# Neighbourhood attention in an order written by hand, with the DeltaNet's branch product as filler work

## The chip, the cores and the metric

One core of one Trainium2 chip. The metric is the device time of one execution in microseconds (us), the median of several runs. The core has five engines that run their own instruction queues in order: TensorE (PE, matrix products, with its weight loads listed apart as PEld), VectorE (DVE), ScalarE (ACT), GpSimd (POOL) and SyncE (SP, which only issues transfers here). ACT and POOL issue transfers too.

## The reference

One layer of a flow-matching model, D_MODEL = 1024, for T = 640 tokens: 128 context tokens and 512 latent tokens on a grid of 8 rows by 64 columns. In every layer a DeltaNet branch and an attention branch read the same normalised input, and their outputs are merged:

```python
def _merge(o_na, o_dn, z, gate_na, gate_dn, dn_norm, w_ao, w_do, w_out):
    o_dn = _rms(o_dn, dn_norm) * jax.nn.silu(z).reshape(B, T, DN_HEADS, DN_DV)
    br_na = o_na.reshape(B, T, NA_WIDTH) @ w_ao
    br_dn = o_dn.reshape(B, T, DN_V_WIDTH) @ w_do
    m = jax.nn.sigmoid(gate_na) * br_na + jax.nn.sigmoid(gate_dn) * br_dn
    return m @ w_out
```

The attention has 8 heads of 64. A context token attends to the 128 context tokens. A latent token attends to a window of 8 rows by 16 columns of the grid, with a relative bias, and to 128 cached context keys, under one softmax. Queries and keys of the latent tokens are rotated by their grid position first. A feed-forward part (squared ReLU, hidden width 4096) follows. All is float32.

## The kernel before

Every dense product is done as three products of float32r parts: `hi*hi + hi*lo + lo*hi`, so a weight is loaded (`load_raw`, SP), copied to `whi` (`S.copy`, ACT) and subtracted to `wlo` (DVE). What the text calls a step is three matmuls with one weight tile.

The order of instructions comes in two ways. Inside `tc.manual_schedule(engines={...})` the named engines keep the order of the program text. Elsewhere a planner orders each engine's instructions from its own model of their durations.

The DeltaNet's recurrence is in the first kind. It goes in slots: `slot(...)` runs a part of the recurrence and then takes steps from a generator `dense()` until 2.4 nominal us are reached (a step is counted as its columns at full clock). `dense()` goes through units of projection weights listed in `FILL`: `v` (values), `q` (queries and keys), `g` (gates, 16 units of 16 steps of 320 columns), with `m` and `a` small extras. A function can be put off by some slots with `later(slots, phase, f)`, run by `do(phase)`; the phases of a slot are "mid", "end", "post". After the last recurrence step the slots go on until all units are done (L1123). Each of the last two steps has a normalisation of the DeltaNet's output (`finish_o`: squares, norms, product, transposes `turned`, store to `od_d` in DRAM).

Then comes the attention, ordered by the planner. Its loops go over four pairs of heads `hp` and five blocks `b`: four latent blocks of 128 queries, which are 16 columns by 8 rows, with 256 window keys and 128 cached ones, and one context block. A pair's two heads lie in the partitions 0 to 63 and 64 to 127. Per head and block: scores into PSUM (L1207 and L1209; L1212 for the context block), the bias added and the minimum found in one DVE instruction (L1227; the scores are negated, so this is the softmax's maximum), the exponential with its sum (ACT, L1231), the reciprocal (L1232) and the normalisation (DVE, L1233), three transposes by PE (L1236) and their copy to `pT` (ACT, L1238). Then the values of both heads (L1250) and the split of the output into `aoh` and `aol`. The rotations of queries and keys are DVE instructions (L1181 to L1192), with the products with the tables on POOL for all pairs but the first. POOL also negates the bias. Values `vw` are loaded by SP, queries, keys and bias by ACT.

The branch products are two passes over `w_br`: i = 1 is the DeltaNet's (reads `doh`, `dol`; L1309 writes `dop`), i = 0 the attention's (reads `aoh`, `aol`), which also adds the two and splits the sum for the next product. Each pass has four weight tiles of two halves, and for each half 384 and 256 columns. All three lines L202, L203, L204 are the helper `mm3`. The planner puts the first pass among the attention; the second pass follows the attention, and the product with `w_out` follows that.

Of the kernel before, what the change touches and what calls it, by code (L numbers as in the profile page):

```python
# [18 lines left out]
P = 128  # L19
D = 1024  # L20
KT = 8
# [7 lines left out]
FILL = ("qv", "vqmqmqmqmqmqmqmgmgagagagagagagaggagggggg")  # L29
# [68 lines left out]
def body(ctx: ExitStack, tc: tile.TileContext, I, O, dbg=None):  # L98
# [47 lines left out]
    def newton_rsqrt(pool, x, n, tag, post=1.0):  # L146

        y = pool.tile([P, n], F32, tag=tag + "y", name=tag + "y")
        t = pool.tile([P, n], F32, tag=tag + "t", name=tag + "t")
        i = pool.tile([P, n], I32, tag=tag + "i", name=tag + "i")  # L150
# [730 lines left out]
    def finish_o(ot, hv, rq, rq2, home):  # L881

        def squares():
# [5 lines left out]
            later(len(home) > 2, "end", lambda: norms(fz, zt))  # L889

        def norms(fz, zt):
            s8 = tk.tile([P, 8], F32, tag="fs8", name="fs8", bufs=2)
            V.tensor_reduce(s8, h8(fz), axis=AX.X, op=ALU.add)
            V.tensor_tensor(s8, s8, rq2, op=ALU.mult)
            V.tensor_scalar(s8, s8, EPS, None, op0=ALU.add)
            rs = newton_rsqrt(tk, s8, 8, "fo")
            V.tensor_tensor(rs, rs, rq, op=ALU.mult)
            later(1, "end", lambda: product(rs, zt))

        def product(rs, zt):  # L900
            V.tensor_tensor(h8(zt), h8(zt), bch(rs), op=ALU.mult)
            hold[2] = V.tensor_tensor(ot, ot, zt, op=ALU.mult).ins
            later(4 if len(home) == 2 else 3 if home else 1, "mid", lambda: turned(zt))
# [15 lines left out]
    class Unit:  # L919
        def __init__(self, ch, i):  # L920
            self.ch, self.i, self.extra = ch, i, []
            self.src = I[dict(v="w_v", q="w_qk", g="w_gate")[ch]][i]
# [9 lines left out]
        def sub(self):  # L932
            for raw, (hi, lo) in zip(self.raw, self.w):
                V.tensor_tensor(lo, raw, hi.bitcast(F32), op=ALU.subtract)  # L934
            kt = 4 if self.ch == "v" else 8
# [7 lines left out]
        def out(self, g, ps, n):  # L943
# [10 lines left out]
            else:  # L954
                hp, mi = i // 2, i % 2
                S.activation(y, ps, AF.Copy, scale=(-0.125 if mi == 0 else 1.0))
# [5 lines left out]

        def run(self):
            for g in range(5 if self.ch == "v" else 2):
# [38 lines left out]
    cnts = dict.fromkeys("vqgma", 0)  # L1003
    prs, elims, plan = [], [], {}
    hold = [None] * 4
    now = [0]
# [4 lines left out]
    def do(phase):  # L1011
        for f in plan.pop((now[0], phase), ()):
            f()
# [16 lines left out]
    def dense():  # L1030
        for j, u in enumerate(us):
            if j + 1 < len(us):
                us[j + 1].load_extra()
            if j + 3 < len(us):
                us[j + 3].load()
            if j + 1 < len(us):
                us[j + 1].cast()
                later(0, "post", us[j + 1].sub)
# [7 lines left out]
    with tc.manual_schedule(engines={E_.PE, E_.DVE, E_.Activation, E_.SP}):  # L1046
# [36 lines left out]
        for n in range(5):  # L1083
            P0, P1, P2 = [preps[i] if i < 5 else none for i in (n, n + 1, n + 2)]
# [37 lines left out]
        raw3[0] = None  # L1122
        while slot() or plan:  # L1123
            pass
# [16 lines left out]

    with (
        tc.tile_pool(name="at0", bufs=2, side="right", reuse_waits="tile") as at0,
        tc.tile_pool(name="at", bufs=2, side="right", reuse_waits="tile") as at,
    ):
        def load_vw(hp):
            vw = at0.tile([P, 4, 2, 256], F32, tag="vw", name="vw", bufs=1)
            for b in range(4):
                for kt in range(2):
                    nc.sync.dma_start(vw[:, b, kt], v_rc[4 * kt : 4 * kt + 4, W0[b] : W0[b] + 32, hp * 128 : hp * 128 + 256])  # L1150
            return vw

        W0 = (0, 8, 24, 32)
        v_rc = v_d.rearrange("t p e -> (t p) e")[128:640].rearrange("(r c) e -> r c e", c=64)
        vw = load_vw(0)
        rope = at0.tile([P, 1024], F32, tag="rope", name="rope", bufs=1)
        nc.scalar.dma_start(rope, I["rope"])
        ckT = at0.tile([P, HP, 128], F32, tag="ckT", name="ckT", bufs=1)
        nc.scalar.dma_start(ckT, I["ckT"])
        cvt = at.tile([P, 512], F32, tag="cvt", name="cvt", bufs=1)  # L1160
        nc.scalar.dma_start(cvt, I["cv"])
        vctx = at.tile([P, 512], F32, tag="vctx", name="vctx", bufs=1)
        nc.scalar.dma_start(vctx, v_d[0])
        bias = [(at0, at)[i // 2].tile([P, 384], F32, tag=f"bias{i}", name=f"bias{i}", bufs=1) for i in range(4)]
        for b in bias:
            V.memset(b[:, 256:384], 0.0)
        swap = [16 + i for i in range(16)] + list(range(16))
        bi, bth = [0, 1], [None, None]
        for hp in range(HP):
            if hp == 2:  # L1170
                vw = load_vw(2)
            RE = V if hp == 0 else G

            rx = ExitStack()
            for ins in hold[2 * hp : 2 * hp + 2]:
                rx.enter_context(tc.issue_after(ins))
            for mi in range(2):
                x = at0.tile([P, T], F32, tag=f"qk{mi}", name=f"qk{mi}", bufs=(1, 2)[mi])
                nc.scalar.dma_start(x, qk_d[hp, mi])
                xs = at0.tile([P, 512], F32, tag="xs", name="xs", bufs=1)  # L1180
                V.stream_shuffle(xs, x[:, 128:640], swap)  # L1181
                V.tensor_tensor(xs, xs, rope[:, 512:1024], op=ALU.mult)
                if mi == 0:
                    qb = at0.tile([P, T], F32, tag="qb", name="qb")
                    S.copy(qb[:, 0:128], x[:, 0:128])
                    RE.tensor_tensor(x[:, 128:640], x[:, 128:640], rope[:, 0:512], op=ALU.mult)
                    V.tensor_tensor(qb[:, 128:640].rearrange("p (b r c) -> p r b c", r=8, b=4),
                                    x[:, 128:640].rearrange("p (r b c) -> p r b c", r=8, b=4),
                                    xs.rearrange("p (r b c) -> p r b c", r=8, b=4), op=ALU.add)
                else:  # L1190
                    RE.tensor_tensor(x[:, 128:640], x[:, 128:640], rope[:, 0:512], op=ALU.mult)
                    V.tensor_tensor(x[:, 128:640], x[:, 128:640], xs, op=ALU.add)  # L1192
                    kT = x
            rx.close()
            oh_g, ol_g = [x[:, hp, 128:640].rearrange("p (r b c) -> p b r c", r=8, b=4) for x in (brh[0], brl[0])]


            for b in range(5):
                nk = 384 if b < 4 else 128
                nj = nk // 128  # L1200
                hh = [slice(0, 64), slice(64, 128)]
                sps = [ps_tp() for _ in range(2)]
                if b < 4:
                    for hs, ps in zip(hh, sps):
                        kg = kT[hs, 128:640].rearrange("p (r c) -> p r c", r=8)
                        lq = qb[hs, 128 + 128 * b : 256 + 128 * b]
                        PE.matmul(ps[:, 0:256].rearrange("p (r c) -> p r c", r=8), lq, kg[:, :, W0[b] : W0[b] + 32], start=True, stop=True)  # L1207
                    for hs, ps in zip(hh, sps):
                        PE.matmul(ps[:, 256:384], qb[hs, 128 + 128 * b : 256 + 128 * b], ckT[hs, hp, :], start=True, stop=True)  # L1209
                else:  # L1210
                    for hs, ps in zip(hh, sps):
                        PE.matmul(ps[:, :128], qb[hs, 0:128], kT[hs, 0:128], start=True, stop=True)  # L1212
                pTs = []
# [646 lines left out]
```

## Time and profile before

| what | us |
|---|---|
| median of 3 runs (1145.94 to 1147.84) | 1147.3 |
| the profiled execution | 1145.61 |
| its span, first to last instruction | 1143.7 |
| PE busy | 1076.5 (94%) |
| PE weight loads busy | 947.5 (83%) |
| DVE busy | 862.4 (75%) |
| ACT busy | 525.7 (46%) |
| POOL busy | 306.6 (27%) |

The mean granted clock of PE was 0.986 of full speed. The last recurrence step of the DeltaNet ends on PE at about 489 us from the span's start, the last attention matmul is at 623.4, and the attention's branch product runs from 625.6 to 660.5. Busy shares of PE are to be read with care: matmuls are pipelined, a listed duration is a matmul's latency, and the distance of two starts is what it costs.

### The profile page before, as it was taken

To read this page: it belongs to the slowest core of one execution; us is meant where nothing else is said; L and a number is where in the kernel's file an instruction comes from. 1 tells how busy PE (TensorE), PEld (TensorE's weight loads), DVE (VectorE), ACT (ScalarE), POOL (GpSimd) and SP (SyncE) were. 2 spreads that over 40 slices of the span, in tenths; PEclk is the share of its full clock that TensorE was granted. 3 is DMA by queue.
4 is the path that set the end of the run, shared out by engine and by line. 5 is a ranking of instruction groups with operands and counts; after the bars stand their busy time and mean duration, and the time that the engine had idled before them with its cause. 6 is when DMAs were issued, how large, how long until landed. Compare 5 with 4: busy or idle time off the path is not lost.

```text
span 1143.7 us, 25017 instructions
## 1 busy us (share of the span) xinstructions
PE 1076.5 (94%) x10016; PEld 947.5 (83%) x10016; DVE 862.4 (75%) x1687; ACT 525.7 (46%) x1154; POOL 306.6 (27%) x238
## 2 busy tenths in 40 slices
PE   4999999989989899989999999999999999999996
PEld 2779999878867788877877999998989888897975
DVE  6567897596777777577655667699798989879785
ACT  5435443426353553434446353476444454444532
POOL 1352312000000000003220405435353534535213
PEclk9998999999989999998999999999999999999999
DMA  8831114555654544566333562446555565665605
GB/s 306 307 125 56 26 37 141 191 179 196 192 194 155 190 129 156 153 192 195 93 104 131 193 258 93 129 117 179 147 148 166 148 163 154 164 165 146 177 28 148
DMA packets 75061, 176.39 MB, mean 154 GB/s; under 512 B 16952, under 2 KB 31048, under 8 KB 74944
## 3 DMA queue, kind: packets, MB, share of 16 engines
q1 hardware_dynamic: 57136, 134.60, 35.2%
q0 software_dynamic: 4928, 15.08, 7.8%
q10 hardware_dynamic: 12880, 25.10, 6.9%
q8 instruction: 79, 1.29, 0.5%
q14 instruction: 38, 0.31, 0.1%
HBM read 150.63 MB, written 24.12 MB: 153 GB/s over the span
## 4 chain that ended last, share of the span: by engine, by line
PE 68%; DVE 17%; DMA 6%; ACT 4%; issue 3%; SPq 0%; POOL 0%; DVEq 0%; ACTq 0%; POOLq 0%
PE ps_mm L968 5%; PE ps_mm L970 4%; PE ps_mm L969 4%; DVE wlo L183 4%; PE ps_mm L203 3%; PE ps_mm L202 3%; PE ps_mm L204 3%; PE ps_mm L1460 3%; PE ps_mm L1458 2%; PE ps_mm L1459 2%; DVE y L523 2%; DVE R L1571 2%; PE ps_st L1460 2%; PE ps_st L1458 2%; PE ps_st L1459 2%
## 5 line engine op out<-in xcount | busy, mean ns | idle before, releaser
L968 PE MATMUL ps_mm<-hhi,whi 128*128 128x320 f32 x384 | 128.7, 335 | 7.7 <-ACT gth L947 4.0
L970 PE MATMUL ps_mm<-hhi,wlo 128*128 128x320 f32 x384 | 119.9, 312 | 2.0 <-DVE wlo L934 2.0
L969 PE MATMUL ps_mm<-hlo,whi 128*128 128x320 f32 x384 | 119.8, 312 | 0.0
L182 ACT CAST whi<-raw 128x1024 fp32r<-128x1024 f32 x89 | 92.3, 1046 | 39.3 <-PE ps_mm L1459 7.3
L183 DVE TENSOR_TENSOR wlo<-raw,whi 128x1024 fp32r<-128x1024 f32 x66 | 86.6, 1322 | 25.5 <-ACT whi L182 25.1
L968 PEld LDWEIGHTS ps_mm<-hhi,whi 128*128 128x128 f32 x384 | 73.5, 191 | 21.6 <-ACT gth L947 8.7
L1223 POOL TENSOR_SCALAR bias<-bias 128x256 f32<-128x256 f32 x24 | 22.1, 927 | 226.6 <-DMA bias<-in_bias_dram 210.0
L183 POOL TENSOR_TENSOR wlo<-raw,whi 128x1024 fp32r<-128x1024 f32 x23 | 56.1, 2442 | 84.6 <-ACT whi L182 84.6
L970 PEld LDWEIGHTS ps_mm<-hhi,wlo 128*128 128x128 f32 x384 | 73.3, 191 | 2.3 <-DVE wlo L934 2.3
L969 PEld LDWEIGHTS ps_mm<-hlo,whi 128*128 128x128 f32 x384 | 73.5, 191 | 0.1
L202 PE MATMUL ps_mm<-hhi,whi 128*128 128x320 f32 x192 | 60.9, 317 | 0.0
L203 PE MATMUL ps_mm<-hlo,whi 128*128 128x320 f32 x192 | 60.6, 316 | 0.0
L204 PE MATMUL ps_mm<-hhi,wlo 128*128 128x320 f32 x192 | 60.1, 313 | 0.0
L183 DVE TENSOR_TENSOR wlo<-S,whi 128x1024 fp32r<-128x1024 f32 x28 | 54.8, 1973 | 3.9 <-ACT whi L182 3.9
L183 DVE TENSOR_TENSOR wlo<-T,whi 128x1024 fp32r<-128x1024 f32 x28 | 44.0, 1570 | 15.3 <-ACT whi L182 15.3
L659 POOL DMA_DIRECT2D rls<-ai_d x10 | 5.1, 510 | 181.5 <-PE ps_tb L622 167.9
L934 DVE TENSOR_TENSOR wlo<-raw,whi 128x1024 fp32r<-128x1024 f32 x28 | 34.2, 1226 | 23.1 <-ACT whi L930 22.7
L182 ACT CAST whi<-T 128x1024 fp32r<-128x1024 f32 x28 | 29.4, 1049 | 33.4 <-PE ps_mm L1459 15.8
L523 DVE SCALAR_TENSOR_TENSOR y<-cvb,cw,y 128x644 f32<-128x644 f32 x48 | 42.6, 887 | 0.9
L182 ACT CAST whi<-S 128x1024 fp32r<-128x1024 f32 x28 | 28.9, 1051 | 22.3 <-PE ps_tb L204 10.7
L947 ACT ACTIVATE gth<-ps_mm 128x320 f32<-128x320 f32 x32 | 13.8, 435 | 51.5 <-PE ps_mm L970 42.3
L202 PEld LDWEIGHTS ps_mm<-hhi,whi 128*128 128x128 f32 x192 | 36.7, 191 | 0.8 <-ACT cvb L519 0.3
(576 smaller groups left out, 3580.7 us busy)
## 6 DMA issues: line engine op xcount, KB each, us to landing
raw<-in_w_ff_dram SPq DMA_DIRECT2D x57, 512.0 KB
raw<-in_w_ada_dram SPq DMA_DIRECT2D x48, 512.0 KB
raw<-in_w_gate_dram SPq DMA_DIRECT2D x16, 512.0 KB
S<-in_w_ff_dram SPq DMA_DIRECT2D x14, 512.0 KB
T<-in_w_ff_dram SPq DMA_DIRECT2D x14, 512.0 KB
S<-in_w_ff_dram POOLq DMA_DIRECT2D x14, 512.0 KB, 5.5
T<-in_w_ff_dram POOLq DMA_DIRECT2D x14, 512.0 KB, 7.3
raw<-in_w_dn_dram SPq DMA_DIRECT2D x12, 512.0 KB
```

Source lines behind the costliest of these rows:

```text
L182: S.copy(hi, raw)
L183: eng.tensor_tensor(lo, raw, hi.bitcast(F32), op=ALU.subtract)
L202: PE.matmul(out, ah, bh, start=(i == 0), stop=False)
L203: PE.matmul(out, ah, bl, start=False, stop=False)
L204: PE.matmul(out, al, bh, start=False, stop=(i == n - 1))
L523: V.scalar_tensor_tensor(y, b[:, j : j + 644], cw[:, mt * 5 + j : mt * 5 + j + 1], y, op0=ALU.mult, op1=ALU.add)
L968: PE.matmul(ps, ah, bh, start=(k == 0), stop=False)
L969: PE.matmul(ps, ah, bl, start=False, stop=False)
L970: PE.matmul(ps, al, bh, start=False, stop=(k == KT - 1))
L1458: PE.matmul(o, hi[:, k, fs], bh, start=(first and k == 0), stop=False, skip_group_check=not first)
L1459: PE.matmul(o, hi[:, k, fs], bl, start=False, stop=False, skip_group_check=not first)
L1460: PE.matmul(o, lo[:, k, fs], bh, start=False, stop=(k == 3), skip_group_check=not first)
```

## The change

- `FILL` gets four units `d` (the DeltaNet's branch product, `Unit.branch`) and three units `n` (weights of the attention's branch product, only loaded, cast and subtracted). The fourth tile is loaded as before.
- The slots after the last DeltaNet step go on only until the put-off functions are done (`while plan: slot()`); the gate units that are left stay in the generator.
- The attention goes under `manual_schedule` for PE, DVE, ACT and SP. A loop over j from -2 to 20 makes 23 turns. In turn j the engines get: scores of block j+2, sums of j+1, transposes of j, bias and exponentials of j+2, normalisation of j+1, values of j-1, two steps of a rotation for a later pair, and 1.5 nominal us of `dense()`. Both heads' scores are issued next to each other, as are their transposes and values.
- Scores are no longer negated: the reduction takes the maximum, a small DVE instruction a block negates it, and POOL's negation of the bias goes. One head of a pair is normalised by ACT (`sums`), the other by DVE (`norm`). The context block uses the same instruction with a bias of zero. The four latent blocks of a pair share a PSUM bank for their outputs, which are split once a pair.
- The rope products of POOL go to DVE. Values, queries and keys of later pairs, bias from the third load on, the DeltaNet's outputs `oraw` and the later gates are loaded from POOL's queue.
- The norms of the DeltaNet's last two steps are done together (16 columns instead of twice 8).
- `raw3`, a third raw weight buffer, is given up at the start of the last recurrence pair (n == 4), and in the turns the subtraction of a unit's weights comes one turn later (`late`).
- The second pass of the branch product takes its weights ready from the units `n`, and its gates from up to three buffers filled ahead (`next_g`).

```diff
-FILL = ("qv", "vqmqmqmqmqmqmqmgmgagagagagagagaggagggggg")
+FILL = ("qv", "vqmqmqmqmqmqmqmgmgagagagagagagaggagggggg" + "ddddnnn")
...
-            later(len(home) > 2, "end", lambda: norms(fz, zt))
+            if not home or len(home) > 2:
+                both[:] = [(tk.tile([P, 16], F32, tag="fs8", name="fs8", bufs=2), [])]
+            s16, xs = both[0]
+            i = slice(8 * len(xs), 8 * len(xs) + 8)
+            xs.append((zt, rq, product))
+            def sums():
+                V.tensor_reduce(s16[:, i], h8(fz), axis=AX.X, op=ALU.add)
+                V.tensor_tensor(s16[:, i], s16[:, i], rq2, op=ALU.mult)
+                if not home:
+                    norms(s16, xs)
+                elif len(xs) == 2:
+                    later(0, "post", lambda: norms(s16, xs))
+            later(0, "end", sums)
...
+        def branch(self):
+            assert len(turned_o) == HP
+            whi, wlo = self.w[0]
+            for mi in range(2):
+                j = 2 * self.i + mi
+                g = gs[j]
+                next_g()
+                ms = slice(mi * 128, mi * 128 + 128)
+                for sl in (slice(0, 384), slice(384, 640)):
+                    w = sl.stop - sl.start
+                    ps = ps_mm()[:, :w]
+                    for k in range(HP):
+                        PE.matmul(ps, whi[:, k, ms], brh[1][:, k, sl], start=(k == 0), stop=False)
+                        PE.matmul(ps, whi[:, k, ms], brl[1][:, k, sl], start=False, stop=False)
+                        PE.matmul(ps, wlo[:, k, ms], brh[1][:, k, sl], start=False, stop=(k == HP - 1))
+                        if k == HP - 1:
+                            V.scalar_tensor_tensor(dop[:, j, sl], g[:, sl], 1.0, ps, op0=ALU.add, op1=ALU.mult)
+                        yield 3 * w / 2400
...
+    def next_g():
+        j = len(gs)
+        if j < 2 * KT:
+            p, n = (mg3, 1) if j > KT and (j - KT) % 3 == 2 else (mg, 2)
+            gs.append(p.tile([P, T], F32, tag="gl", name="gl", bufs=n))
+            (nc.sync if j <= KT else nc.gpsimd).dma_start(gs[j], gt_d[2 * (j % KT) + (j < KT)])
...
+            if n == 4:
+                raw3[0] = None
...
-        raw3[0] = None
-        while slot() or plan:
-            pass
+        while plan:
+            slot()
...
+        def exps(j):
+            hp, b = BLK[j]
+            nk = width(j)
+            sts[j] = st = at.tile([P, 8], F32, tag="st", name="st", bufs=4)
+            prs_[j] = [at.tile([P, 384], F32, tag="pr", name="pr", bufs=6) for _ in range(2)]
+            for hq, ps in enumerate(sps[j]):
+                bt = bias[(3 * hp + (0, 1, 1, 2)[b]) % 2][hq] if b < 4 else bias[0][hq][:, 256:384]
+                V.tensor_tensor_reduce(prs_[j][hq][:, :nk], ps[:, :nk], bt, 1.0, -3.0e38, ALU.add, ALU.max, st[:, hq : hq + 1])
+            V.tensor_scalar(st[:, 6:8], st[:, 0:2], -1.0, None, op0=ALU.mult)
+            for hq in range(2):
+                x = prs_[j][hq][:, :nk]
+                S.activation(x, x, AF.Exp, bias=st[:, 6 + hq : 7 + hq], accum_out=st[:, 2 + hq : 3 + hq])
+        def sums(j):
+            nk, st = width(j), sts[j]
+            V.reciprocal(st[:, 4:6], st[:, 2:4])
+            S.activation(prs_[j][1][:, :nk], prs_[j][1][:, :nk], AF.Copy, scale=st[:, 5:6])
+        def norm(j):
+            nk, st = width(j), sts[j]
+            V.tensor_scalar(prs_[j][0][:, :nk], prs_[j][0][:, :nk], st[:, 4:5], None, op0=ALU.mult)
...
+        with tc.manual_schedule(engines={E_.PE, E_.DVE, E_.Activation, E_.SP}):
+            late[0] = 1
+            rot, oraw, subs = rotations(1, xq), [], []
+            for j in range(-2, n + 1):
+                hp, b = BLK[min(j + 2, n - 1)]
+                if j + 2 < n:
+                    scores(j + 2)
+                if 0 <= j + 1 < n:
+                    sums(j + 1)
+                if 0 <= j < n:
+                    turned(j)
+                if j + 2 < n:
+                    exps(j + 2)
+                    m = 3 * hp + (2, None, 3, 4, None)[b] if b in (0, 2, 3) else 99
+                    if m < 12:
+                        load_bias(m, nc.gpsimd)
+                if 0 <= j + 1 < n:
+                    norm(j + 1)
+                while subs:
+                    subs.pop(0)()
+                if j in (0, 2):
+                    oraw = []
+                    for i in range(2):
+                        oraw.append(mg.tile([P, T], F32, tag="gl", name="oraw", bufs=2))
+                        nc.gpsimd.dma_start(oraw[i], od_d[len(turned_o) + i])
+                if 0 <= j - 1 < n:
+                    values(j - 1)
+                    if BLK[j - 1][1] > 2:
+                        out(j - 1)
+                    if BLK[j - 1][1] == 4 and BLK[j - 1][0] < 2:
+                        load_vw(BLK[j - 1][0] + 2)
+                if j in (1, 3):
+                    for x in oraw:
+                        i = len(turned_o)
+                        S.copy(brh[1][:, i], x)
+                        subs.append(lambda i=i, x=x: V.tensor_tensor(brl[1][:, i], x, brh[1][:, i].bitcast(F32), op=ALU.subtract))
+                        turned_o.append(i)
...
+                for _ in range(2):
+                    next(rot, None)
+                if b == 4 and j + 2 < n - 5:
+                    rot = rotations(hp + 2, [load_x(hp + 2, mi, nc.gpsimd) for mi in range(2)]) if hp + 2 < HP else none
+                slot(us=1.5)
...
-        for i in (1, 0):
...
-            for c in range(4):
-                whi, wlo = load_w(I["w_br"][i, c], HP, 256)
...
+    wbr = [u.w[0] for u in us[-3:]] + [load_w(I["w_br"][0, 3], HP, 256)]
+    for c in range(4):
+        whi, wlo = wbr[c]
```

More of the change, by code (lines that the diff above doesn't have):

```diff
@@ L1011, in do @@
     def do(phase):
-        for f in plan.pop((now[0], phase), ()):
-            f()
+        while (now[0], phase) in plan:
+            for f in plan.pop((now[0], phase)):
+                f()
     for u in units(FILL[0]):
@@ L1037, in dense @@
                 us[j + 1].cast()
-                later(0, "post", us[j + 1].sub)
+                later(late[0], "post", us[j + 1].sub)
+            if j + 3 < len(us) and not raw3[0]:
+                if late[0]:
+                    later(late[0], "post", us[j + 3].load)
+                else:
+                    us[j + 3].load()
             yield from u.run()
@@ L1160, in body @@
+        for i in range(2):
+            for b in bias[i]:
+                V.memset(b[:, 256:384], 0.0)
+        load_vw(0)
+        load_bias(0, nc.scalar)
+        rx = ExitStack()
+        for ins in hold[0:2]:
+            rx.enter_context(tc.issue_after(ins))
+        for mi in range(2):
+            for _ in rotate(0, mi, xq[mi]):
+                pass
+        rx.close()
         cvt = at.tile([P, 512], F32, tag="cvt", name="cvt", bufs=1)
-        nc.scalar.dma_start(cvt, I["cv"])
         vctx = at.tile([P, 512], F32, tag="vctx", name="vctx", bufs=1)
-        nc.scalar.dma_start(vctx, v_d[0])
@@ new lines, in body, with rotations, scores @@
+        for x, src in ((cvt, I["cv"]), (vctx, v_d[0])):
+            nc.scalar.dma_start(x, src)
+        load_bias(1, nc.scalar)
+        xq = [load_x(1, mi, nc.scalar) for mi in range(2)]
+        load_vw(1)
+        def rotations(hp, xq):
+            for mi in range(2):
+                yield from rotate(hp, mi, xq[mi])
+        sps, prs_, sts, pTs, pos = {}, {}, {}, {}, {}
+        def scores(j):
+            hp, b = BLK[j]
+            qb, kT = qbs[hp], kTs[hp]
+            sps[j] = [ps_tp() for _ in range(2)]
+            if b < 4:
+                for hs, ps in zip(hh, sps[j]):
+                    kg = kT[hs, 128:640].rearrange("p (r c) -> p r c", r=8)
+                    lq = qb[hs, 128 + 128 * b : 256 + 128 * b]
+                    PE.matmul(ps[:, 0:256].rearrange("p (r c) -> p r c", r=8), lq, kg[:, :, W0[b] : W0[b] + 32], start=True, stop=True)
+                for hs, ps in zip(hh, sps[j]):
+                    PE.matmul(ps[:, 256:384], qb[hs, 128 + 128 * b : 256 + 128 * b], ckT[hs, hp, :], start=True, stop=True)
+            else:
+                for hs, ps in zip(hh, sps[j]):
+                    PE.matmul(ps[:, :128], qb[hs, 0:128], kT[hs, 0:128], start=True, stop=True)
@@ new lines, in values @@
+        def values(j):
+            hp, b = BLK[j]
+            if b in (0, 4):
+                pos[hp] = ps_st(2) if b == 0 else ps_tb()
+            po_ = pos[hp][:, b % 4 * 128 : b % 4 * 128 + 128]
+            nj = width(j) // 128
+            for k in range(nj):
+                for hq, (hs, pT) in enumerate(zip(hh, pTs[j])):
+                    h = 2 * hp + hq
+                    if b == 4:
+                        vv = vctx[:, h * 64 : h * 64 + 64]
+                    elif k == 2:
+                        vv = cvt[:, h * 64 : h * 64 + 64]
+                    else:
+                        vv = vws[hp][:, b, k, hq * 64 : hq * 64 + 64]
+                    PE.matmul(po_[hs], vv, pT[:, k * 128 : k * 128 + 128], start=(k == 0), stop=(k == nj - 1))
```

271 lines of the change are left out of this document (124 added, 147 removed).

## The prediction

> **What bounds the kernel now.** I read the page's first part, then a table of windows around the attention, then TensorE's (PE's) timeline there, the waits, VectorE's (DVE's) and ScalarE's (ACT's) groups, and the POOL queue.
>
> ```profile
> PE 1076.5 (94%) x10016; PEld 947.5 (83%) x10016; DVE 862.4 (75%) x1687; ACT 525.7 (46%) x1154; POOL 306.6 (27%) x238
> ...
> 489.30:525.30 36.00, 31.89 (x216) 30.11 (x213) 27.34 (x68) 13.02 (x24) 6.15 (x5) 1.00 0.69 216
> 525.30:624.30 99.00, 96.94 (x635) 74.41 (x633) 63.86 (x203) 47.84 (x142) 23.02 (x23) 0.97 0.33 104
> 624.30:660.80 36.50, 33.28 (x213) 32.34 (x213) 23.79 (x37) 13.63 (x22) 15.07 (x15) 0.95 0.56 195
> ```
>
> PE is the bound. The three windows (columns: length, then busy time and count of PE, PEld, DVE, ACT, POOL, then granted clock, DMA share, GB/s) are the stages that the change touches: the tail of the DeltaNet with the last gate units (36.0 us), the attention with the DeltaNet's branch product (99.0), the attention's branch product (36.5). Together 171.5 us. In the middle one PE is busy nearly all the time; the timeline shows what that time is made of.
>
> ```profile
> 524.35 0.31 PE L968 MATMUL ps_mm<-hhi,whi 128*128 128x320 f32 x1
> 524.79 0.31 PE L968 MATMUL ps_mm<-hhi,whi 128*128 128x320 f32 x1
> ...
> 602.10 0.33 PE L203 MATMUL ps_mm<-dol,whi 128*128 128x384 f32 x1
> 602.62 0.34 PE L203 MATMUL ps_mm<-dol,whi 128*128 128x384 f32 x1
> 602.89 0.33 PE L1250 MATMUL ps_tb<-pT,vw 128*64 128x128 f32 x2
> ...
> 610.93 0.70 PE L1207 MATMUL ps_tp<-qk,qb 64*128 64x256 f32 x2
> 611.46 0.38 PE L1209 MATMUL ps_tp<-ckT,qb 64*128 64x128 f32 x2
> 611.77 0.55 PE L1236 MATMUL ps_st<-cst,pr 128*128 128x128 f32 x3
> ...
> 613.09 0.71 PE L1207 MATMUL ps_tp<-qk,qb 64*128 64x256 f32 x4
> 613.63 0.39 PE L1209 MATMUL ps_tp<-ckT,qb 64*128 64x128 f32 x4
> 613.95 0.55 PE L1236 MATMUL ps_st<-cst,pr 128*128 128x128 f32 x3
> 614.43 0.66 PE L1250 MATMUL ps_tb<-pT,vw 128*64 128x128 f32 x8
> ...
> 615.23 0.49 PE L1207 MATMUL ps_tp<-qk,qb 64*128 64x256 f32 x2
> 617.41 0.48 PE L1212 MATMUL ps_tp<-qk,qb 64*128 64x128 f32 x2
> 617.83 0.44 PE L1250 MATMUL ps_st<-pT,vw 128*64 128x128 f32 x4
> 623.40 0.91 PE L1250 MATMUL ps_tb<-pT,vctx 128*64 128x128 f32 x4
> 659.18 0.28 PE L202 MATMUL ps_mm<-aoh,whi 128*128 128x256 f32 x1
> 659.53 0.28 PE L202 MATMUL ps_mm<-aoh,whi 128*128 128x256 f32 x1
> ```
>
> Read the starts, not the durations, since matmuls overlap. Three dense matmuls take 0.44 us at 320 columns, 0.52 at 384, 0.35 at 256. One head's scores alone take 0.84 us (610.93 to 611.77); both heads side by side, on the two halves of the array, take 0.86 (613.09 to 613.95). So a pair issued together costs half of two apart, and the planner mostly sets them apart, because each head's scores wait for their own buffer. Three transposes take 0.48, the values of a pair issued together 0.80. A change between dense and attention matmuls costs about 0.10 (602.62 to 602.89 is 0.27, against 0.17).
>
> **The attention on PE in the new order.** Sixteen latent blocks of 0.86 + 2 x 0.48 + 0.80 = 2.62 us: 41.9. Four context blocks of 0.42 + 2 x 0.16 + 0.91 = 1.65: 6.6 (the 0.42 is one head's row; were both heads apart, 0.84, and 1.7 us more in all). Sum 48.5. What it takes now is the remainder of the first two windows, 135.0 us, once the dense work and the waits are taken out.
>
> ```profile
> L968 PE MATMUL ps_mm<-hhi,whi x63: 303/309/418, 489.3 to 524.8; 128*128 128x320 f32 x63
> ...
> PE ps_mm L203 <- DVE dol L1281: 2.0, 1, 2.0
> PE ps_mm L970 <- DVE wlo L934: 2.0, 1, 2.0
> PE ps_mm L968 <- ACT gth L947: 1.7, 1, 1.7
> PE ps_mm L202 <- ACT whi L182: 1.3, 1, 1.3
> PE ps_mm L202 <- DVE gl L1309: 1.3, 1, 1.3
> ...
> 528.00:536.00 8.00, 6.80 (x32) 0.57 0.35 104
> 626.50:631.50 5.00, 4.63 (x21) 0.66 0.81 262
> ```
>
> Gate work: 63 x 0.44 = 27.7. Branch product: 4 units x 2 halves x 4 steps of three at each width: 32 x 0.52 + 32 x 0.35 = 27.8. Waits: 2.0 + 2.0 + 1.7 = 5.7. Clock: after the wait for `dol` 8 us ran at 0.57, a loss of 8 x 0.43 = 3.4. Remainder 135.0 - 27.7 - 27.8 - 5.7 - 3.4 = 70.4 us for an attention that costs 48.5 when heads go in pairs, plus changes. That gap is what a hand-written order can win.
>
> **The change, part by part, on PE from 489.3 on.**
> Dense work: the same 27.7 + 27.8. Counting the steps, the DeltaNet's five last slots and the slot before them take 36 gate steps, the turns the other 27 and all of the branch product; at 1.5 nominal us a turn it lasts into the last of the 23 turns (j from -2 to 20), so almost no turn is bare.
> Changes: into and out of the dense part, 23 x 2 x 0.10 = 4.6 (the others are inside the 2.62).
> Sum of work: 27.7 + 27.8 + 48.5 + 4.6 = 108.6.
> The Trainium skill, TensorEngine Tiling (Array Packing), Key Properties, says that a change of tiling mode drains the engine; by that rule each of the 46 changes would cost a matmul's latency beyond its cadence, estimated from the quoted 384-column row as 0.33 - 0.17 = 0.16 us, and the sum would be 2.8 higher. The trace's 0.10 decides here.
>
> Waits left: (a) In the slots, 3.7 now. The two norms become one chain of small DVE instructions in place of two, so DVE is freer for `wlo`; against it the third raw buffer goes one step earlier, and SP (the DMA queue of SyncE) then holds a load until `wlo` is subtracted, with the DeltaNet's own loads behind it, at most a slot of six gate steps, 2.6. Between 0 and 6.3 I take 2, nearest to the `wlo` row. (b) DVE's backlog from the first rotation: the first scores' reduction can wait though PE does not; 0 to 5 rotations of 0.69 (row below), I take 3. (c) In the turns.
>
> ```profile
> L1227 DVE CUSTOM_DVE_ANT_0 s<-ps_tp,bias 128x384 f32<-128x384 f32 x32 | 17.5, 552 | 11.7 <-PE ps_tp L1209 11.6
> L1233 DVE TENSOR_SCALAR pr<-pr,st 128x384 f32<-128x384 f32 x32 | 13.7, 427 | 1.0
> L1232 DVE RECIPROCAL st<-st 128x1 f32<-128x1 f32 x40 | 6.4, 159 | 9.1 <-ACT pr L1231 9.1
> L183 DVE TENSOR_TENSOR wlo<-raw,whi 128x1024 fp32r<-128x1024 f32 x4 | 4.9, 1218 | 2.0 <-ACT whi L182 2.0
> L1192 DVE TENSOR_TENSOR qk<-qk,xs 128x512 f32<-128x512 f32 x3 | 2.1, 692 | 1.4 <-POOL qk L1191 1.2
> L1231 ACT ACTIVATE pr<-s,st 128x384 f32<-128x384 f32 x32 | 19.8, 617 | 16.6 <-DVE st L1227 16.3 <-DVE st L1232 0.4
> ```
>
> DVE in the turns: its 63.9 of the middle window, less half the normalisations, 16 x 0.43 = 6.9 (they go to ACT), plus six rope products from POOL and three rotation steps that lay before the window, 9 x 0.69 = 6.2, plus six more weight subtractions, 7.3, plus twenty one-column sign changes, 3.2: 74. PE has 11.9 + 27.8 + 48.5 + 4.6 = 92.8 there. A full turn is 2.62 + 1.7 + 0.2 = 4.5 on PE. In order on DVE it is reciprocal 0.16, two reductions 1.10, sign 0.16, one normalisation 0.43, two rotation steps 1.38 in half the turns, a product's exit of about 0.5 and, every fourth turn, a subtraction 1.22: 2.4 to 3.7, 5.0 with the subtraction. The loop of reduction, sign, exponentials (two of 0.62) and reciprocal is 2.7, and it has two turns until its transposes. So PE leads, the branch product has two PSUM buffers for DVE's late turns, and I take 4 us of waits, between 0 and the 30 that I come to with the rival.
> What is gone: the wait for `dol` and the slow stretch after it, as `dol` is made in the turns j = 2 and 3 and used from j = 4 on, under gate steps.
> New length: 108.6 + 2 + 3 + 4 = 117.6 against 135.0: 17.4 less.
>
> **The third window.** 192 matmuls of the branch product, 27.8, and 213 - 192 = 21 of the next product at 0.12, 2.5; 1 us for the last output's split; 1 for a wait. 32.3 against 36.5: 4.2 less. The weights come ready from the turns, so the 1.3 for `whi` goes; the gates have three buffers, so the 1.3 for `gl` mostly goes; with them the stretch at 0.66, 5 x 0.34 = 1.7. Casts and subtractions of these weights (3 x 1.22 on DVE) are hidden in the turns; without that cover they cost at most 3.7.
> Everything behind keeps its order and its loads, which start as much earlier: nothing.
> The sum is 21.6 less. The profiled execution has 1145.6 around its span of 1143.7, 1.7 under the median 1147.3. From the median: 1125.7.
>
> **POOL's queue.** About 60 loads of the turns (values, bias, queries, outputs) are issued from POOL, where SP and ACT did it.
>
> ```profile
> L659 POOL DMA_DIRECT2D rls<-ai_d x10: 497/500/537, 112.9 to 338.6; - x10
> ...
> DMA to landing us min/median/max: 1.8/2.4/5.4
> ```
>
> 60 x 0.50 = 30 us in some 100, on an engine that loses its rope products and sign changes. A bias buffer is refilled three turns, 13 us, ahead of use: 2 x 0.5 of issue behind eight value loads of 0.5 and 5.4 to land is 10.4. I take nothing; cover 2.6. The Trainium skill, SBUF — State Buffer, Who interferes with whom, says that DVE's two-port instructions lock POOL out while it writes descriptors; no row of the trace shows a load delayed so, and a normalisation of 0.43 would be the longest such hold in a turn.
>
> **Rivals.**
> *All cover holds* (no waits a, b, c): 9 less, 1117. For it: PE leads each turn by 0.8 or more. Against: the start has DVE full. 0.12.
> *DVE sets the turns' pace.* Its waits in the middle window, 11.6 for scores and 9.1 for exponentials, with about 10 for the rest, stay: 74 + 30 = 104 in place of 92.8 + 4, so 7 more, 1133. For it: DVE waits for PE's product at the end of each turn and then for the next scores. Against: two PSUM buffers. 0.13.
> *Part is given back behind*: merged weights and gates meet the loads of the next products at the window's end; the stalls of the third window return, 5 to 8 us: 1132. 0.08.
> *POOL's queue is late* (the other side). It works in order: a load that waits for its buffer holds the bias behind it. If ten bias pairs each come late by 4 us (the 5.4 landing twice, less the cover), that is 40, with PE idle and its clock down as at 528; 1166. It decides from 2.2 us a pair. For it: values, queries and bias share one queue. Against: three turns of lead. 0.09.
> *No change that shows* (paired scores don't come to run together, so 16 x 0.82 = 13 of the 21.6 is lost, with the rest in waits): 1146. 0.03.
>
> **Numbers.** My forecast has 0.55, with 1118 to 1134 as its own range; the rivals as given. Faster by over 0.2% (what a measurement of this kernel can tell from no change): 0.55 + 0.12 + 0.13 + 0.08 = 0.88; within: 0.03; slower: 0.09. From 1110 (all cover and the turns' changes free) to 1141 leaves out the last two and a little below.
>
> **What would show it.** Scores in fours, 0.86 from the first to the transposes, in nearly all 16 blocks; the attention's stage at 110 to 120 us from the same point of the last slot; no wait for `dol`, no clock under 0.9 there; turns of about 4.5 us; the third window near 32. Wrong if DVE's idle time in the turns lies before the reciprocal while PE waits for PSUM, or if DVE's reductions wait for the bias from POOL's queue.

## The result, and the profile after

The changed kernel takes 1116.6 us (median of 6, 1113.6 to 1122.6) against 1146.6 for the kernel before (median of 6 beside it): a ratio of 0.975, 95% interval 0.971 to 0.980. The forecast was 1126, in a range of 1110 to 1141. The measured time lies in that range, but under the 1118 to 1134 that the prediction gave as its forecast's own; it is the time of the rival "all cover holds", 1117, which had 0.12.

The profiled execution has 1113.6 around a span of 1111.6, against 1143.7 for the span before. First the page's line of busy times, then the three windows (length; busy time and count of PE, PEld, DVE, ACT, POOL; granted clock, DMA share, GB/s), then three rows of PE's timeline that mark the stage's ends: the DeltaNet's last product, the last attention matmul, the last matmul of the attention's branch product.

```profile
PE 1053.6 (95%) x10016; PEld 932.6 (84%) x10016; DVE 850.9 (77%) x1657; ACT 529.8 (48%) x1162; POOL 316.5 (28%) x275
...
490.40:510.40 20.00, 19.79 (x142) 19.12 (x138) 17.53 (x47) 7.06 (x16) 1.16 (x2) 1.00 0.59 176
510.40:595.00 84.60, 84.60 (x705) 71.33 (x704) 60.54 (x192) 57.85 (x158) 24.66 (x42) 1.00 0.53 163
595.00:631.00 36.00, 35.21 (x240) 33.76 (x239) 26.15 (x41) 13.46 (x24) 20.84 (x23) 1.00 0.55 187
...
489.40 1.15 PE L864 MATMUL ps_st<-vn,KQ 64*64 64x64 f32 x32
594.57 0.44 PE L1348 MATMUL ps_tb<-pT,vctx 128*64 128x128 f32 x4
628.32 0.28 PE L202 MATMUL ps_mm<-aoh,wlo 128*128 128x256 f32 x1
```

From the DeltaNet's last product to the last attention matmul is 594.57 - 489.40 = 105.2 us; before it was 623.40 - 488.26 = 135.1. From there to the last matmul of the branch product 33.8 against 37.1. Together 33.3 less; the stage starts 1.1 later, so the span is 32.1 shorter, and nothing comes back behind. (The 1.1 says little: in two executions of the changed kernel the stage starts at 489.4 and at 497.1.) PE has no gap at all in the turns (84.60 of 84.60), and the clock is whole in all three windows. One turn on PE:

```profile
516.65 0.70 PE L1289 MATMUL ps_tp<-qk,qb 64*128 64x256 f32 x4
517.19 0.39 PE L1291 MATMUL ps_tp<-ckT,qb 64*128 64x128 f32 x4
517.51 0.87 PE L1328 MATMUL ps_st<-cst,pr 128*128 128x128 f32 x6
518.31 0.66 PE L1348 MATMUL ps_st<-pT,vw 128*64 128x128 f32 x8
518.80 0.39 PE L1348 MATMUL ps_st<-pT,cvt 128*64 128x128 f32 x4
519.12 0.41 PE L1004 MATMUL ps_mm<-hhi,whi 128*128 128x320 f32 x1
519.37 0.31 PE L1005 MATMUL ps_mm<-hlo,whi 128*128 128x320 f32 x1
...
520.84 0.31 PE L1006 MATMUL ps_mm<-hhi,wlo 128*128 128x320 f32 x1
521.08 0.49 PE L1294 MATMUL ps_tp<-qk,qb 64*128 64x128 f32 x4
```

From start to start: scores 0.86, six transposes 0.80, values 0.81, then twelve dense matmuls: 4.43 in all. The longest of PE's waits from 480 to 660 are these (engine, line, what it waited for; total, times, longest). Only the first is over 0.3. It ends at 485.5, ahead of the whole stage, and it is new: the last row is the kernel before at the same product.

```profile
PE ps_st L831 <- issue: 2.3, 1, 2.3
PE ps_st L202 <- DVE mlo L1466: 0.3, 1, 0.3
...
PE ps_st L833 <- issue: 0.4, 1, 0.4
```

### The profile page after: what moved, and what is told of

It is laid out like the page before. It is cut to its first block, busy times and chain, and to the rows that moved or that the text cites. A ratio compares the mean times of both kernels' runs of the same rounds, so it can differ in the third digit from the quotient of the medians.

```text
span 1111.6 us, 24906 instructions
## 1 busy us (share of the span) xinstructions
PE 1053.6 (95%) x10016; PEld 932.6 (84%) x10016; DVE 850.9 (77%) x1657; ACT 529.8 (48%) x1162; POOL 316.5 (28%) x275
## 4 chain that ended last, share of the span: by engine, by line
PE 70%; DVE 19%; ACT 5%; issue 4%; DMA 1%; DVEq 0%; ACTq 0%; SPq 0%
PE ps_mm L1004 6%; PE ps_mm L1006 5%; PE ps_mm L1005 5%; DVE wlo L181 4%; PE ps_mm L1613 3%; PE ps_mm L200 3%; PE ps_mm L1612 3%; PE ps_mm L1611 3%; PE ps_mm L201 2%; PE ps_mm L202 2%; DVE y L521 2%; DVE R L1724 2%; PE ps_st L1612 2%; PE ps_st L1611 2%; PE ps_st L1613 2%
## 5 line engine op out<-in xcount | busy, mean ns | idle before, releaser
L180 ACT CAST whi<-raw 128x1024 fp32r<-128x1024 f32 x82 | 85.1, 1046 | 32.7 <-PE ps_mm L1612 8.5
L1004 PEld LDWEIGHTS ps_mm<-hhi,whi 128*128 128x128 f32 x384 | 74.4, 194 | 20.3 <-ACT gth L961 6.2
L200 PE MATMUL ps_mm<-hhi,whi 128*128 128x320 f32 x192 | 60.5, 315 | 0.6 <-ACT cvb L517 0.6
L201 PE MATMUL ps_mm<-hlo,whi 128*128 128x320 f32 x192 | 59.7, 311 | 0.0
L1213 POOL DMA_DIRECT2D vw<-v_d x32 | 21.1, 668 | 134.7 <-issue 96.6
L944 ACT CAST whi<-raw 128x1024 fp32r<-128x1024 f32 x35 | 36.5, 1046 | 7.0 <-issue 6.1
L180 ACT CAST whi<-S 128x1024 fp32r<-128x1024 f32 x28 | 28.8, 1051 | 22.6 <-PE ps_tb L202 11.1
```

Of the source, the lines that this page charges most:

```text
L180: S.copy(hi, raw)
L200: PE.matmul(out, ah, bh, start=(i == 0), stop=False)
L201: PE.matmul(out, ah, bl, start=False, stop=False)
L1004: PE.matmul(ps, ah, bh, start=(k == 0), stop=False)
```

## The experiments

Stage S runs from the start of the DeltaNet's last product to the start of the last attention matmul, W from there to the last matmul of the attention's branch product, both in the profiled execution. S does not hold the 2.3 us wait, which ends before it. Ratios are to the kernel before, timed beside each run. The edits are shown shortened.

| kernel | us (median) | ratio, 95% interval | S | W |
|---|---|---|---|---|
| before | 1146.6 | 1 | 135.1 | 37.1 |
| changed | 1116.6 | 0.975 (0.971 to 0.980) | 105.2 | 33.8 |
| changed, again | 1118.5 | 0.974 (0.969 to 0.980) | 105.1 | 33.7 |
| heads apart as written | 1121.2 | 0.978 (0.974 to 0.983) | 109.3 | 33.8 |
| heads split by other work | 1146.1 | 1.000 (0.998 to 1.002) | 135.3 | 33.7 |
| planner's order | 1142.6 | 0.996 (0.994 to 0.999) | 128.6 | 34.1 |
| bare turns | 1135.1 | 0.989 (0.986 to 0.993) | see text | 32.6 |
| one more DVE sum a turn | 1118.1 | 0.975 (0.970 to 0.979) | 105.5 | 33.8 |
| three more | 1130.2 | 0.985 (0.980 to 0.991) | 117.6 | 34.2 |
| weights late | 1120.9 | 0.979 (0.974 to 0.983) | 104.9 | 36.7 |
| turns' loads on SP | 1121.2 | 0.979 (0.976 to 0.981) | 109.8 | 34.2 |
| loads off ACT | 1116.6 | 0.974 (0.971 to 0.977) | 108.8 | 33.7 |
| values first | 1111.9 | 0.970 (0.968 to 0.973) | 102.2 | 33.8 |
| both | 1114.8 | 0.974 (0.971 to 0.977) | 104.9 | 33.7 |

(W of the bare turns starts at the last dense matmul of the DeltaNet's branch, since there the dense work lies behind the attention.)

What S is made of on PE, for five of the kernels: each matmul of the timeline counts from its start to the next start, less the gaps. (The DeltaNet's own 1.8 to 2.2 us are left out.)

| kernel | scores | transposes | values | dense work | gaps |
|---|---|---|---|---|---|
| before | 26.6 | 14.8 | 20.7 | 65.0 | 6.1 |
| changed | 15.4 | 14.1 | 14.0 | 59.7 | 0.2 |
| heads split by other work | 28.8 | 17.0 | 27.8 | 59.6 | 0.3 |
| planner's order | 26.7 | 15.6 | 17.2 | 62.9 | 4.0 |
| values first | 15.8 | 10.9 | 14.0 | 59.3 | 0.3 |

**Is it the pairing?** The first attempt wrote one head's matmuls before the other's:

```
 scores:  for hs, ps in zip(hh, sps[j]):
              matmul(ps[:, 0:256], ...)          # one head: latent keys,
+             matmul(ps[:, 256:384], ...)        # then its context keys, then the other head
-         for hs, ps in zip(hh, sps[j]):
-             matmul(ps[:, 256:384], ...)
 values:
-   for k in range(nj):
-       for hq ...
+   for hq ...
+       for k in range(nj):
```

> The changed kernel, but in scores and values all matmuls of one head come before those of the other (transposes, order of the turns, filler and loads as they are). Pairing theory (two heads side by side on the array cost about what one costs): scores of a latent block 2 x 0.84 in place of 0.86, 16 x 0.82 = 13.1 us, context scores 4 x 0.42 = 1.7; values have no row with the heads apart, but carry 384 columns a head as the scores do, so 1.4 to 1.6 in place of 0.80, 10 to 13 us. Turns 84.6 -> 109 to 113 us, whole kernel about 1142 (1136 to 1146), nearly all of the gain gone. Rival (the hand order and the filler brought the gain; which head stands where is hidden): turns 85 to 90 us, 1117 to 1122.

It missed: 109.3 in S, 4.2 more than the changed kernel. The timeline of this run says why:

```profile
515.02 0.71 PE L1289 MATMUL ps_tp<-qk,qb 64*128 64x256 f32 x4
515.56 0.39 PE L1290 MATMUL ps_tp<-ckT,qb 64*128 64x128 f32 x4
515.88 0.88 PE L1327 MATMUL ps_st<-cst,pr 128*128 128x128 f32 x6
...
520.11 0.71 PE L1347 MATMUL ps_st<-pT,vw 128*64 128x128 f32 x6
...
521.18 0.42 PE L1004 MATMUL ps_mm<-hhi,whi 128*128 128x320 f32 x1
```

The scores still take 0.86 (515.02 to 515.88): although the program has one head's context scores ahead of the other head's latent ones, the records show all four latent parts first. So here the array takes both heads' scores side by side in either written order. The values take 1.07 in place of 0.81, and 16 x 0.26 = 4.2 is the whole loss. So the edit had not separated the heads, and said nothing against the pairing. The second attempt put other work between them. (In the listing 64\*128 is a matmul on half of the array's rows, 128\*64 on half of its columns, 128\*128 on all of it; going from one kind to another is called a change of the array's division here.)

```
+for q in range(2):
+    scores(j + 2, q); turned(j, q); values(j - 1, q)    # head q alone
-scores(j + 2); turned(j); ...; values(j - 1)            # both heads
```

> The changed kernel, with work of the full array set between the heads: in each turn head 0's scores, transposes and values, then head 1's. Pairing theory, now of two matmuls that can be in the array at once whatever their written order: scores 16 x 0.82 = 13.1 us, context scores 1.7; the values of one head alone, with no row yet, 0.53 to 0.84, so 16 x 0.26 to 0.88 = 4 to 14; 20 turns x 3 more changes x 0.10 = 6. Turns and slots from the last DeltaNet product to the last attention matmul 105.5 -> 130 to 140 us, whole kernel 1142 to 1152. Rival (a pair together is worth little more than the 4 us that the heads-apart run showed): 1120 to 1126.

```profile
524.01 0.70 PE L1291 MATMUL ps_tp<-qk,qb 64*128 64x256 f32 x2
524.54 0.38 PE L1293 MATMUL ps_tp<-ckT,qb 64*128 64x128 f32 x2
524.86 0.55 PE L1331 MATMUL ps_st<-cst,pr 128*128 128x128 f32 x3
525.34 0.65 PE L1351 MATMUL ps_st<-pT,vw 128*64 128x128 f32 x4
525.82 0.38 PE L1351 MATMUL ps_st<-pT,cvt 128*64 128x128 f32 x2
526.13 0.70 PE L1291 MATMUL ps_tp<-qk,qb 64*128 64x256 f32 x2
...
519.00:631.40 112.40, 112.40 (x689) 89.77 (x687) 60.98 (x187) 59.17 (x156) 24.82 (x42) 1.00 0.40 120
```

One head alone: scores 0.85, three transposes 0.48, values 0.79, which is 2.12, and 4.24 for both, against 2.47 (0.86 + 0.80 + 0.81) together. S is 30.2 longer, the middle window has no gap and no loss of clock, and the whole kernel is as slow as the one before. The turns, the filler and the loads are left in place, so this is the price of setting the heads apart: 13.4 in the scores and 13.8 in the values. The other 3.0 are the transposes, which the edit parts too. The changes of the array's division that it adds lie inside these numbers; no run has the heads apart without them. The Trainium skill, TensorEngine Tiling (Array Packing), Key Properties, says that different tiles can load weights and multiply in parallel; the 0.85 and 0.86 agree.

**Does the written order matter, or would any order do?**

```
-with tc.manual_schedule(engines={PE, DVE, Activation, SP}):
+with ExitStack():                                       # the planner orders the turns
```

> The changed kernel, but the turns' instructions are ordered by the planner from its costs instead of staying in the written order; the work is the same. Theory (the written order is what puts the heads together and covers the waits): the planner again sets the heads' scores apart, 0.82 a block, and lets DVE-bound stretches uncovered; turns 84.6 -> 100 to 110 us, 1132 to 1142. Rival (the regrouped work itself, dense steps in the turns, normalisation on ACT and ready weights, brought the gain and any order would do): turns 84 to 90 us, 1116 to 1122.

```profile
496.00:516.00 20.00, 16.27 (x98) 15.05 (x96) 17.71 (x51) 4.48 (x10) 1.68 (x3) 0.87 0.44 139
516.00:536.00 20.00, 19.82 (x114) 17.81 (x113) 10.62 (x30) 12.81 (x28) 2.15 (x4) 0.79 0.52 151
...
605.31 0.70 PE L1289 MATMUL ps_tp<-qk,qb 64*128 64x256 f32 x2
...
606.59 0.70 PE L1289 MATMUL ps_tp<-qk,qb 64*128 64x256 f32 x2
```

1142.6, just above the theory's range: the same work in the planner's order keeps 4 of the 30 us. S is 23.4 longer: 16.0 in the attention's matmuls, 11.3 of that in the scores, 3.8 in gaps and 3.2 in dense work. Nine of the sixteen blocks have their heads one after the other, as at 605.31 and 606.59 (in twos). The lower clock of the first 40 us, at most 20 x 0.13 + 20 x 0.21 = 6.8, is in these numbers. The run undoes the whole order, the filler's places too, and not the heads' alone.

**What is the filler worth?**

```
-slot(us=1.5)
+slot(us=0)                                              # dense steps only after the last turn
```

> The changed kernel, but the turns take no dense steps; the same 24 gate steps and the branch product follow after the last turn. Theory (filler covers the loop of reduction, exponentials and reciprocal, and the copies of the transposes): a bare turn is 3.3 to 3.9 us against 2.46 of PE work, 23 turns 76 to 90, then 38.4 of dense work: 114 to 128 in place of 84.6, so 1146 to 1160. Rival (two turns between scores and transposes are enough cover by themselves, PE sets a bare turn too): 2.5 to 2.7 a turn, 60 + 38.4 = 99 less the full turns' share 46, about 84 to 90 in all, 1117 to 1122.

```profile
516.00:546.00 30.00, 22.25 (x154) 16.63 (x155) 22.51 (x72) 20.78 (x58) 14.41 (x25) 0.77 0.59 182
546.00:579.40 33.40, 30.89 (x282) 22.70 (x281) 22.86 (x94) 29.19 (x88) 10.27 (x17) 1.00 0.21 60
...
PE ps_st L1328 <- ACT pT L1330: 6.3, 3, 5.3
```

1135.1, between the theory (1146 at least) and the rival (1122 at most). The later bare turns take 2.8 us on average (nine in 24.9). PE's own work in a turn, context blocks included, is 2.2 (43.5 in twenty turns), so some waiting is left, but far less than the theory's 3.3 to 3.9. The attention and the dense work together grew by 18.2: the gaps by 10.2 and the attention's matmuls by 11.9, while the dense work, now in one piece, takes 4.0 less. Of the gaps 7.75 lie in the first 30 us, one of them, 5.3, where ACT's copies of the transposes stand behind the DeltaNet's outputs, which come late from memory (ACT waits up to 4.3 for `oraw` there). The lower clock of that stretch, at most 30 x 0.23 = 6.9, is in the 11.9. So two turns of lead cover most of the softmax loop; what the filler covers is above all the late loads at the start, and the clock.

**Does DVE set the pace?** A sum of 128x384 into a scratch tile, once or three times a turn:

```
+for _ in range(1):                                      # or 3
+    V.tensor_tensor(junk, junk, rope[:, 0:384], op=ALU.add)
```

> The changed kernel with one more sum of 128x384 on DVE in each of the 23 turns (into a scratch tile that nothing reads). By the 0.43 of a normalisation and the 0.69 of a 512-column product it is about 0.5 us, 12 in all. PE theory (PE sets the turns, DVE is busy 60.5 of 84.6): the turns stay at 84.6, 0 to 2 us, 1117 to 1120. Rival (DVE's chain sets the pace and PE only looks busy, since a matmul's record stretches over its wait): 8 to 12 us, 1126 to 1131.

> The same with three more sums a turn, about 36 us in all: DVE's work in the turns 60.5 + 36 = 96 against PE's 84.6. PE theory: DVE is now the pace, 96 plus what it must still wait for, turns 96 to 110, 1130 to 1144. Rival (DVE already sets the pace): 36 more, 1150 to 1156. If the kernel stays below 1125, DVE has more room than its busy time shows.

The window of the turns with one sum, then with three:

```profile
507.60:592.50 84.90, 84.81 (x706) 71.36 (x704) 70.14 (x214) 58.33 (x158) 24.59 (x42) 1.00 0.54 161
...
513.00:610.00 97.00, 90.94 (x707) 75.84 (x705) 92.46 (x256) 58.83 (x160) 24.71 (x42) 0.96 0.47 144
```

With one, DVE is busy 70.1 in place of 60.5 and S moves by 0.3. With three DVE is busy 92.5 of 97 and sets the pace; S grows by 12.4. So of the 31.9 us added to DVE some 20 found room in the turns.

**The ready weights.**

```
-FILL ... + "ddddnnn";  wbr = [u.w[0] for u in us[-3:]] + [load_w(...)]
+FILL ... + "dddd";     whi, wlo = load_w(I["w_br"][0, c], HP, 256)      # for all four
```

> The changed kernel without the three weight units of the attention's branch product in the turns; all four are loaded and split at their use, as before. Theory (ready weights are worth the third window's share): the 1.3 us wait for the first cast comes back, with a stretch of lower clock behind it (1.7 in the trace of before) and up to 1 for subtractions: third window 33.5 -> 36 to 37.5, 1121 to 1123; the turns stay, since the three subtractions less on DVE are off the path. Rival (the window is set by PE alone): 0 to 1, 1118 to 1119.

```profile
595.80:632.40 36.60, 34.20 (x220) 33.01 (x219) 26.01 (x39) 13.81 (x22) 19.48 (x22) 0.95 0.63 228
...
PE ps_mm L200 <- ACT whi L180: 1.6, 1, 1.6
```

W is 36.7 in place of 33.8: the wait of 1.6 for the cast is back, and the clock falls to 0.95 (36.6 x 0.05 = 1.8). The trace shows the 3 us; the times (1120.9 against 1118.5) can't tell it from nothing by themselves.

**The queue of the turns' loads.** `nc.gpsimd` to `nc.sync` in four places:

> The changed kernel, with the turns' loads (values, bias, queries and keys, outputs of the DeltaNet) issued on SP's queue, behind and before its weight loads and gate stores, in place of POOL's. Theory (the loads have turns of lead, so the queue doesn't matter): turns and slots 105.5 +- 1 us, 1116 to 1121. Rival (an own queue keeps holds of up to 7 us, which POOL shows before a bias load, away from the weight loads): some weight loads late by 2 to 7 us each, PE waits of 5 to 20, 1124 to 1138.

S is 4.6 longer, between the two theories. The turns are as full as before (85.00 of 85.00); the loss is one wait ahead of them, 3.3 for a gate's exit, with its clock. Against it the 2.3 us wait ahead of S is 0.4 here. Why ACT runs late in this run is not shown. The exit stood on ACT, which had stood 6.81 behind its own issue of cv and stood 2.25 more just ahead of the exit:

```profile
499.04 0.63 ACT L886 ACTIVATE kt<-kt 128x512 f32<-128x512 f32 x1 [6.81 <-DMA cvt<-in_cv_dram]
...
PE ps_mm L1004 <- ACT gth L961: 3.3, 1, 3.3
```

**Two tries at a better kernel.** Loads off ACT (`nc.scalar` to `nc.gpsimd` for the first two bias pairs, cv, the context's values, and the second pair's queries and keys):

> The changed kernel, with five groups of loads before the turns (first and second bias, cv, the context's values, queries and keys of the second pair) issued on POOL in place of ACT. Theory (an issue on ACT that waits for its buffer holds ACT's casts: 7.06 us idle at 481 ahead of a cast, DVE 5.3 behind it, PE 2.3 behind that): the 2.3 us wait of PE goes, 2 to 4 us less, 1113 to 1117. Rival (that wait is DVE's own chain of the last DeltaNet steps): unchanged, 1117 to 1120.

```profile
494.08 0.69 DVE L844 TENSOR_TENSOR kt<-kt,qS 128x512 f32<-128x512 f32 x1 [4.04 <-DMA kt<-o_d]
...
493.00:513.00 20.00, 17.95 (x120) 17.18 (x117) 17.56 (x47) 5.49 (x14) 1.61 (x3) 0.91 0.42 122
```

The wait at the DeltaNet's last step falls from 2.3 to 0.4, but DVE then waits 4.04 for a load of `o_d`, and PE 1.9 at the transposes behind it, with the clock at 0.91: 1.9 won ahead of S, 3.6 lost in it. That the issues on ACT cause the 2.3 is not shown either, since the run on SP's queue has 0.4 there too with these loads still on ACT. The times (1112.3 to 1121.2, the profiled execution the slowest of six) can't tell this kernel from the changed one. Values ahead of the transposes:

```
 scores(j + 2); sums(j + 1)
+values(j - 1)
 turned(j)
 ...
-values(j - 1)
```

> The changed kernel, with the values of the block before ahead of the transposes in each turn, so that the transposes, which use the full array as the dense steps do, stand next to them. Theory of changes (each change of the array's division costs 0.08 to 0.10): one change less a turn, six transposes and the first dense start 0.72 as in the heads-apart run in place of 0.80: 20 x 0.08 = 1.6 us less, turns 83 us, 1115 to 1118. Rival (copies of the transposes come 0.8 later on ACT and the exponentials behind them; or scores beside values change dearly): turns 85 to 90, 1119 to 1124.

```profile
515.87 0.70 PE L1289 MATMUL ps_tp<-qk,qb 64*128 64x256 f32 x4
516.40 0.39 PE L1291 MATMUL ps_tp<-ckT,qb 64*128 64x128 f32 x4
516.72 0.66 PE L1348 MATMUL ps_st<-pT,vw 128*64 128x128 f32 x8
517.21 0.39 PE L1348 MATMUL ps_st<-pT,cvt 128*64 128x128 f32 x4
517.53 0.88 PE L1328 MATMUL ps_st<-cst,pr 128*128 128x128 f32 x6
518.16 0.39 PE L1004 MATMUL ps_mm<-hhi,whi 128*128 128x320 f32 x1
518.39 0.31 PE L1005 MATMUL ps_mm<-hlo,whi 128*128 128x320 f32 x1
...
520.09 0.49 PE L1294 MATMUL ps_tp<-qk,qb 64*128 64x128 f32 x4
```

This is the best kernel run here: a full turn is 4.22 in place of 4.43, S 102.2 in place of 105.2, 1111.9 in the median. The six transposes take 0.63 to a dense matmul, 0.80 to the values: 0.17 less, and the scores take no more for having the values behind them (0.85). So ahead of the values the transposes pay 0.17 that they don't pay ahead of the dense work. That this is the price of changing the array's division fits, but is argued. Over the stage the transposes take 10.9 in place of 14.1. The interval of its ratio overlaps those of the changed kernel, so the 3 us rest on the traces. The prediction had weighed the Trainium skill's rule that a change of mode drains the array (TensorEngine Tiling (Array Packing), Key Properties), estimated at 0.16 a change. For the changes into and out of the dense work its 0.10 was nearer; the 0.17 inside the turn agrees with the rule's 0.16.

> Both edits together, loads off ACT and values ahead of transposes. If both theories hold: 1.6 + 2 to 4 us less than the changed kernel, 1112 to 1115, the stage from the last DeltaNet product to the last attention matmul 104 us. If neither: 1117 to 1124.

Both together: 1114.8, inside the range for "both theories hold", but not for that reason. S is 104.9 with the 1.9 us wait of the loads' edit in it. The reordering's gain is there (the transposes take 10.9 again), the loads' is not.

## Why the prediction was right, and which terms were off

Most of its signs came: scores in fours in all sixteen blocks, no wait for `dol`, no low clock in the stage, turns of 4.43. But its sum was off by more than the result shows. The first two windows were to go from 135.0 to 117.6, and by the same marks they came to 104.5. Against these 13 stand the third window, 1.4 over its sum, and the later start of the stage; and the profiled execution is the fastest of six. So that the rival's 1117 was met is luck in part. Point by point:

- **Pairs.** Right, and the main cause. The remainder of 70.4 us for an attention that costs some 48 in pairs was the reading that carried the forecast. It was too high: from start to start the attention of the kernel before takes 62.2, between the 43.5 of the changed kernel and the 73.6 of the split run. In five of its sixteen blocks both heads' scores already stand together.
- **The attention, 48.5.** Mis-sized by 4.5; it is 44.0. Six transposes in a row take 0.80, not twice 0.48: 16 x 0.16 = 2.6. (Six take 0.63 next to dense work, so three are 0.31, and each 0.48 held 0.17 for the half-array work behind it; the sum counted that twice.) The context block's values were put at 0.91, the duration of a row, though the prediction itself says to read starts; from start to start they take 0.37: 4 x 0.54 = 2.2. Its transposes, 0.37 and not 0.32, give 0.2 back.
- **Changes, 4.6.** Right in size: 516.42 to 516.65 is 0.23 into the scores and 519.12 to 519.37 is 0.25 out of the values, against 0.147.
- **Waits, 9.** The step that failed; in these windows they are 0.2. (a) and (b) did not come. (c) took 4 as a middle between 0 and 30, though the sum itself had PE ahead by 0.8 a turn. Its load of DVE was too high as well: 74 for 23 turns, where DVE has 66.7 from the first turn's reduction on (502.3 to 595; the 60.5 above start with the second turn). Left out were that one reciprocal now serves both heads (3.2 in place of 6.0) and that outputs are split once a pair (3.6 in place of 5.4). But the load does not explain the miss: one more sum a turn has DVE busy for 0.83 of the turns, more than the 74 of 92.8 that was foreseen, and S grows by 0.3. What the sum did not have is the new wait of 2.3 ahead of the stage, 0.4 before.
- **Third window, 32.3.** 33.7 from the last attention matmul's end. The last two dense steps of the DeltaNet's branch lie behind that mark, 0.8, which the sum had in the window ahead; the other 0.6 is not traced. The ready weights are worth 3, as the late weights show.
- **POOL's queue.** Right that PE and DVE don't wait for it, though it stands still a lot. The turns' window has 42 issues on it, not 60. Of all waits in the turns, these two show it (engine, line, for what; total, times, longest): POOL's bias issue waits for its buffer, and DVE's reductions wait for PE, never for the bias.

```profile
POOL bias L1245 <- DVE st L1307: 16.0, 5, 7.0
...
DVE pr L1307 <- PE ps_tp L1291: 8.9, 8, 1.8
```

Where the 33 us came from, by the table of S: 18.7 from the attention's matmuls (scores 11.2, values 6.7, transposes 0.8), 5.9 from gaps, 5.3 from dense work, and 3.3 from the third window. The prediction's split had 70.4 - 44.0 - 4.6 = 21.8 for pairs and 9 for waits and clock. The slow stretch behind 528 lies in the dense work and the attention both, so the line between pairs and clock is not exact. The runs that undo one part each lose 30.2 (heads split) and 18.2 (no filler) in the trace. These don't add up to 33, and need not: before, some blocks were paired and some dense work lay between them already.

## What to carry to other kernels

Two half-array matmuls come for about the price of one only while no other work stands between them. Their written order made no difference for the scores here and 0.26 a block for the values, so write them in turns. Price a turn from starts in a trace, and count each change of the array's division, also those inside the block: put work of the same division side by side. Where one engine leads a turn by a clear margin, as PE did here by 0.8 of 4.5, a safe middle for the others' waits was further off than none at all; look for waits at the start instead, where loads come late.

## What the runs showed of the hardware

Scores of two heads on the two halves of the array take 0.86 in either written order (0.86 in the heads-apart run too), and the records show the second head's latent part ahead of the first head's context part. Values, which share rows and split columns, do not forgive it: 1.07 against 0.81.

What a short gap on PE costs in clock varies from run to run. Behind the 2.3 us gap of the changed kernel the clock stayed whole; around the same 1.9 us gap it was 0.86 in the run with loads off ACT and 1.00 in the run with both edits, which is the same program up to there (columns as in the windows above):

```profile
485.50:493.50 8.00, 8.00 (x102) 7.67 (x103) 5.01 (x9) 1.37 (x2) 0.00 (x0) 1.00 0.79 256
...
501.10:513.10 12.00, 10.11 (x63) 9.68 (x62) 10.54 (x33) 3.50 (x10) 1.07 (x2) 0.86 0.47 157
...
499.60:511.60 12.00, 10.11 (x74) 9.68 (x73) 10.96 (x33) 3.80 (x10) 1.38 (x3) 1.00 0.47 153
```

The Trainium skill, TensorE: Matmul & The Clock Gate, Part 1: The HAM clock gate, has the clock judged in windows that run freely, and dropped after an idle one of about 3.4 us. Free-running windows would make it chance whether a gap counts, and the rows fit that; but the drop here came behind a gap of 1.9 us, shorter than that. No run here was made to test either.
